# A modulation vector product moved from three blocks in the first layer into 24 steps between the dense chunks of both layers

## The chip, the cores and the metric

The kernel runs on one core of a Trainium2 chip. The metric is the device time of one execution in microseconds (us); lower is better. Engines are named as the profile names them: PE is the matrix engine (PEld its weight loads), DVE the vector engine, ACT the scalar engine, POOL the general one, SP the engine that issues most DMAs. Each engine works through its own list of instructions in order.

## The reference, cut to what matters

Two blocks follow each other. The first has two layers (an RWKV branch, a sparse attention branch "dsa", a dilated attention branch "dil", an output product, a gate). The second has one layer: attention and a gated delta rule, then 16 experts. Only the second block uses the modulation vector `mod`, and `mod` depends on nothing but the input `c` and its weights:

```
x = first_block(x, ...)                        # DEPTH = 2 layers
mod = jax.nn.silu(c) @ w_ada[l] + b_ada[l]     # [1, 1024] @ [1024, 6144], DEPTH_2 = 1
sh1, sc1, gt1, sh2, sc2, gt2 = split(mod, 6)
h  = rmsnorm(x, norm1_w) * (1 + sc1) + sh1
x  = x + gt1 * hybrid_mixer(h, ...)
h2 = rmsnorm(x, norm2_w) * (1 + sc2) + sh2
x  = x + gt2 * expert_choice_ffn(h2, ...)
```

`w_ada` is 25 MB in f32; it is read once, for one row of output. So the product may be made anywhere ahead of the second block.

## The kernel before

All weights of dense products pass through `wring`, four slots of [128, 1024] f32 (`NW = 4`), which `wraw` fills by DMAs from SP. For a product in halves, `w` lets `split` turn a slot into a high and a low f16 part (ACT writes the high one, DVE the low one) in one of `NS = 3` buffers `w`. `fm` makes one **chunk** of 128 features for 512 tokens from such a buffer: 8 times `mm`, three f16 matmuls each, so 24 matmuls of 512 columns into one accumulator tile `bm`. In a layer 29 chunks are made by `fm`: two for the index queries and one for the index keys, one for `wd`, four (`r`, `k`, `v`, `g`) for each of the three head pairs p of the RWKV branch, nine in `dil`, four in `dsa`.

`emit_rwkv` goes over p = 0, 1, 2. For each it makes the four chunks, prepares the operands (lines 428 to 503: transposes `bt`, products `bg`, masked copies), calls `between(p, 1)`, then `solve` (two triangular systems, six levels, line 325), then the state products and the output `y`. `between` also places the index blocks and `dil` by the table `ORDER`. After the branches come the products with `w_out`, the projection `ple_proj`, the norm of the gate and the gate itself (`dense`).

The modulation is made by `Mod.group`, called from `between` by the table `ADA`: in the first layer only, at p = 0, 1, 2, after the preparation and ahead of `solve`. One group makes 4 x 512 outputs: eight times it loads two [128, 1024] f32 pieces of `w_ada` **through `wring`**, and multiplies them by one column of `sc` (silu of c): four f32 matmuls with one output row each, on rows 0, 32, 64 and 96 of one `bm` tile, which runs on over all eight. Then ACT copies the four rows out and SP stores them. `finish`, called after both layers, adds the bias and turns the vector into columns.

The order in which instructions stand is not the order of the code: a scheduler takes them by their place in the code as priority, as soon as it thinks their inputs and buffers are there, and a tile gets its space in SBUF or PSUM when it is scheduled. So the next p's chunks are put between the steps of the present p's `solve`.

## Time and profile before

| | |
|---|---|
| median of 3 runs | 2205.38 us (2202.47 to 2209.64) |
| profiled execution | 2194.62 us |
| its span, first to last instruction | 2192.8 us |
| PE busy | 2017.3 us (92%) |
| DVE busy | 1303.9 us (59%) |
| ACT busy | 962.3 us (44%) |
| moved by DMA | 348.48 MB, mean 159 GB/s |

PE is busy nearly throughout, so the thing to read is, stretch by stretch, what PE does and for what it waits where it doesn't. Matmuls overlap: what one occupies is read from the start of one to the start of the next, not from its own duration. An f32 matmul has two records in the trace. Both layers run the same code but for the groups, so the layers can be laid over each other by a landmark that both have: line 266, which writes the transposed normed input (`hT0H`) at the start of a layer and again at the norm of the gate. "PEclk" is the granted TensorE clock as a share of full speed (its levels are 1.2 and 2.4 GHz).

### The profile page before, as it was taken

How to read it: one execution, taken by the hardware profiler on the slowest of the kernel's cores; microseconds unless marked ns; L12 is line 12 of the kernel's file. 1: busy time of each engine (PE TensorE's matmuls, PEld its weight loads, DVE VectorE, ACT ScalarE, POOL GpSimd, SP SyncE). 2: the span in 40 equal slices, each digit the busy share in tenths (PEclk: the TensorE clock that was granted, in tenths of full speed). 3: DMA queues.
4: the chain of work that ended last, by engine and by line, in shares of the span. 5: the costliest groups of instructions: out<-in, count | busy, mean ns of one | idle time of the engine just before them, and what ended most of it. 6: DMA issues, size and time to landing. Idle time of an engine off the chain costs nothing. (4 is left out here: it accounts for less than half of the span.)

```text
span 2192.8 us, 31685 instructions
## 1 busy us (share of the span) xinstructions
PE 2017.3 (92%) x12269; PEld 1090.4 (50%) x12273; DVE 1303.9 (59%) x2491; ACT 962.3 (44%) x1839; POOL 234.6 (11%) x266
## 2 busy tenths in 40 slices
PE   6898899989989889989799989899996999999998
PEld 4453445444646545444446555565633444444443
DVE  5787966546689986646768576868566112222221
ACT  5454536444555546444667676757521111011010
POOL 0022131000120231000021020302000000000000
PEclk9999999999999999999999999999998999999999
DMA  6344341043321111044221211111067799999996
GB/s 212 125 135 159 110 157 46 14 163 116 98 96 39 39 49 40 12 157 141 79 77 40 67 40 39 54 52 46 30 212 300 303 403 409 409 409 409 408 409 254
DMA packets 114335, 348.48 MB, mean 159 GB/s; under 512 B 19820, under 2 KB 20604, under 8 KB 114184
## 3 DMA queue, kind: packets, MB, share of 16 engines
q1 hardware_dynamic: 110152, 340.51, 42.1%
q10 hardware_dynamic: 4032, 5.95, 0.8%
q8 instruction: 97, 1.59, 0.3%
q14 instruction: 54, 0.44, 0.1%
HBM read 332.70 MB, written 10.56 MB: 157 GB/s over the span
## 5 line engine op out<-in xcount | busy, mean ns | idle before, releaser
L201 PEld LDWEIGHTS <-w 128*128 128x128 f16 x2472 | 232.7, 99 | 240.9 <-issue 35.3
L201 PE MATMUL bm<-hT0H,w 128*128 128x512 f16 x760 | 256.1, 385 | 0.8 <-DVE w L195 0.4
L201 PE MATMUL bm<-hT1H,w 128*128 128x512 f16 x760 | 251.5, 382 | 0.0
L195 DVE SCALAR_TENSOR_TENSOR w<-wring,w 128x1024 f16<-128x1024 f32 x137 | 179.2, 1312 | 22.7 <-ACT w L192 22.1
L1405 PE MATMUL bm<-wm,xe 128*64 128x512 f32 x848 | 185.4, 593 | 0.0
L192 ACT ACTIVATE w<-wring 128x1024 f16<-128x1024 f32 x137 | 144.4, 1059 | 12.7 <-DMA wring<-in_win 8.9
L201 PE MATMUL bm<-hT0L,w 128*128 128x512 f16 x380 | 146.5, 385 | 0.0
L201 PE MATMUL bm<-hT1L,w 128*128 128x512 f16 x380 | 145.6, 383 | 0.0
L1405 PEld LDWEIGHTS bm<-wm,xe 128*64 128x64 f32 x848 | 75.1, 136 | 106.5 <-issue 99.9
L346 DVE TENSOR_TENSOR Z<-bz,perm 128x512 f16<-128x512 f32 x168 | 108.4, 683 | 24.6 <-PE bz L325 23.3
L356 ACT ACTIVATE XX<-bz 128x512 f16<-128x512 f32 x168 | 106.9, 641 | 6.3 <-PE bz L325 6.1
L1382 DVE TENSOR_SCALAR OH<-phA,perm 128x64 f32<-128x64 f32 x128 | 30.1, 308 | 127.4 <-PE bz L1393 96.8
L325 PEld LDWEIGHTS <-XX 128*128 128x128 f16 x1008 | 73.1, 100 | 65.2 <-DVE XX L340 28.5
L1405 PE MATMUL bm<-wm,aT 128*64 128x512 f32 x432 | 102.3, 602 | 0.7
L616 ACT ACTIVATE PT<-bt 128x128 f32<-128x128 f32 (+3 forms) x112 | 47.9, 430 | 118.7 <-PE bt L614 117.4
L353 ACT ACTIVATE XX<-bz 128x512 f16<-128x512 f32 x140 | 90.1, 643 | 14.7 <-PE bz L325 14.4
L1396 ACT ACTIVATE xe<-bz,perm 128x128 f32<-128x128 f32 x64 | 25.8, 453 | 130.2 <-PE bz L1393 118.9
L311 DVE SCALAR_TENSOR_TENSOR hid<-hth,bm 128x512 f32<-128x512 f32 x16 | 10.3, 683 | 115.8 <-ACT hth L310 115.8
L1393 PEld LDWEIGHTS bz<-OH,x 128*128 128x128 f32 x512 | 62.4, 197 | 29.0 <-issue 26.8
L310 ACT ACTIVATE hth<-bm 128x512 f32<-128x512 f32 x16 | 8.7, 595 | 154.4 <-PE bm L1405 154.4
L1393 PE MATMUL bz<-OH,x 128*128 128x128 f32 x512 | 68.6, 287 | 1.7 <-DVE OH L1382 1.7
L325 PE MATMUL bz<-XX,Z 128*128 128x128 f16 x672 | 66.0, 219 | 3.7 <-ACT XX L353 3.6
(517 smaller groups left out, 4046.6 us busy)
## 6 DMA issues: line engine op xcount, KB each, us to landing
wm<-in_w_up SPq DMA_DIRECT2D x112, 512.0 KB, 10.2
wm<-in_w_down SPq DMA_DIRECT2D x108, 512.0 KB, 10.2
wm<-in_w_gate SPq DMA_DIRECT2D x100, 512.0 KB, 10.2
wring<-in_win SPq DMA_DIRECT2D x95, 512.0 KB, 3.3
wring<-in_w_ada SPq DMA_DIRECT2D x48, 512.0 KB, 3.9
wring<-in_w_gate SPq DMA_DIRECT2D x20, 512.0 KB, 10.2
wring<-in_w_down SPq DMA_DIRECT2D x20, 512.0 KB, 9.8
wring<-in_w_out SPq DMA_DIRECT2D x16, 512.0 KB, 5.3
```

The lines of the kernel that those rows point to most:

```text
L192: d = self.A.activation(out=hi, in_=t, func=AF.Copy, scale=scale)
L195: self.V.scalar_tensor_tensor(out=lo, in0=t, scalar=scale, in1=hi, op0=ALU.mult, op1=ALU.subtract)
L201: self.T.matmul(out, a[i], b[j], start=(start and n == 0), stop=(stop and n == 2))
L325: T.matmul(b[:, u], lhs[:, u], rhs if len(rhs.shape) == 2 else rhs[:, u], start=True, stop=True)
L346: V.tensor_tensor(out=z, in0=mm(HL[j][0], X[j]), in1=lv(systems[j], l, 0), op=ALU.mult)
L353: A.activation(out=X[j], in_=mm(XT[j], Z[j]), func=AF.Copy)
L356: A.activation(out=XT[j], in_=b, func=AF.Copy)
L616: K.A.activation(out=PT[:, :n], in_=b[:, :n], func=AF.Copy)
L1382: V.tensor_scalar(out=y[:, t, 64 * e:64 * e + 64], in0=K.c("iota")[:, 1:65], scalar1=slot[:, t, x:x + 1], scalar2=scale(t, x), op0=ALU.is_ ...
L1393: T.matmul(b[:, j], K.x[t][:, (k0 + j) * 128:(k0 + j + 1) * 128], OH[:, t], start=(t == 0), stop=(t == 3))
L1396: A.activation(out=xe[:, k], in_=b[:, j], func=AF.Identity, scale=n2[:, k:k + 1], bias=modc[:, 24 + k:25 + k])
L1405: T.matmul(bb[hf][s], lhs[:, k, s], w[:, hf * 512:(hf + 1) * 512], start=(k == 0), stop=(k == 7))
```

## The change

`ADA` and `Mod.group` are gone. `fm` calls `Mod.tick` after each chunk, and every second tick is a `step`: it multiplies the pieces that were loaded by the step before (four f32 matmuls), and starts the two loads for the next step. There are 24 steps (three groups of eight k as before), all in the two layers of the first block. The pieces go into tiles `aw` of their own ([128, 2, 1024] f32, two buffers) and no longer through `wring`. Each load is made to wait (`K.after`) for the last matmul of the chunk behind which it stands. `finish` would do what is left over.

```
--- before.py
+++ after.py
@@ -28,7 +28,6 @@
 NS = 3
 ND = 4
 ORDER = {(0, 0): ("1",), (1, 0): ("2",), (2, 0): ("3",), (2, 1): ("dil",), "end": ("dsa", "fin")}
-ADA = {(0, 0, 1): (0,), (0, 1, 1): (1,), (0, 2, 1): (2,)}
 NM = 24
 NM1 = 8
 NC = 4
@@ -198,7 +197,8 @@
     def mm(self, out, a, b, start, stop):
 
         for n, (i, j) in enumerate(((0, 0), (0, 1), (1, 0))):
-            self.T.matmul(out, a[i], b[j], start=(start and n == 0), stop=(stop and n == 2))
+            d = self.T.matmul(out, a[i], b[j], start=(start and n == 0), stop=(stop and n == 2))
+        return d
 
     def wm(self, src, pool):
 
@@ -278,7 +278,8 @@
 
         b = (pool or self.pm).tile([128, 512], F32, name="bm", bufs=4)
         for k in range(8):
-            self.mm(b, tuple(w[:, k * 128:(k + 1) * 128] for w in wt), hT[k], k == 0, k == 7)
+            d = self.mm(b, tuple(w[:, k * 128:(k + 1) * 128] for w in wt), hT[k], k == 0, k == 7)
+        self.mod.tick(d)
         return b
 
     def rope_fm(self, sp, b, cos, sin, mask, out, perm=None, half=None, scale=1.0):
@@ -835,8 +836,6 @@
     later.update(dil=dil, dsa=dsa, **{str(b): (lambda b=b: block(b)) for b in (1, 2, 3)})
 
     def between(p, end):
-        for n in ADA.get((i, p, end), ()):
-            K.mod.group(sp, n)
         for n in ORDER.get((p, end), ()):
             later[n]()
 
@@ -912,6 +911,7 @@
 class Mod:
 
 
+
     def __init__(self, K):
         A, V = K.A, K.V
         self.K = K
@@ -922,25 +922,42 @@
         V.tensor_scalar(out=self.sc, in0=self.sc, scalar1=0.5, scalar2=None, op0=ALU.mult)
         self.c = K.small("modc", 48)
         self.scr = K.dp.tile([12, 512], F32, name="mod")
-
-    def group(self, sp, g):
-
+        self.n, self.calls, self.w = 0, 0, None
+
+    def tick(self, mark):
+        self.calls += 1
+        if self.calls % 2:
+            self.step(mark)
+
+    def step(self, mark=None):
         K = self.K
-        b = K.pm.tile([128, 512], F32, name="bm", bufs=4)
-        for k in range(8):
-            w = [K.wraw(K.a["w_ada"][k * 128:(k + 1) * 128, m * 1024:(m + 1) * 1024]) for m in (2 * g, 2 * g + 1)]
+        if self.w is not None:
+            g, k = divmod(self.n - 1, 8)
+            if k == 0:
+                self.b = K.pm.tile([128, 512], F32, name="bm", bufs=4)
             for j in range(4):
-                d = K.T.matmul(b[32 * j:32 * j + 1], self.sc[:, k:k + 1], w[j // 2][:, (j % 2) * 512:(j % 2) * 512 + 512],
-                               start=(k == 0), stop=(k == 7))
-                if j < 2:
-                    K.after(d, K.wlast)
-        row = sp.tile([128, 512], F32, name="modrow")
-        for j in range(4):
-            K.A.activation(out=row[32 * j:32 * j + 1], in_=b[32 * j:32 * j + 1], func=AF.Copy)
-            K.nc.sync.dma_start(self.scr[4 * g + j:4 * g + j + 1], row[32 * j:32 * j + 1])
+                K.T.matmul(self.b[32 * j:32 * j + 1], self.sc[:, k:k + 1], self.w[:, j // 2, (j % 2) * 512:(j % 2) * 512 + 512],
+                           start=(k == 0), stop=(k == 7))
+            if k == 7:
+                row = K.wp.tile([128, 512], F32, name="modrow")
+                for j in range(4):
+                    K.A.activation(out=row[32 * j:32 * j + 1], in_=self.b[32 * j:32 * j + 1], func=AF.Copy)
+                    K.nc.sync.dma_start(self.scr[4 * g + j:4 * g + j + 1], row[32 * j:32 * j + 1])
+            self.w = None
+        if self.n < 24:
+            g, k = divmod(self.n, 8)
+            self.w = K.wp.tile([128, 2, 1024], F32, name="aw", bufs=2)
+            src = K.a["w_ada"][k * 128:(k + 1) * 128, g * 2048:(g + 1) * 2048].rearrange("p (m n) -> p m n", m=2)
+            for m in range(2):
+                d = K.nc.sync.dma_start(self.w[:, m], src[:, m])
+                if mark is not None:
+                    K.after(d, mark)
+            self.n += 1
 
     def finish(self, sp):
 
+        while self.n < 24 or self.w is not None:
+            self.step()
         K = self.K
         m48 = sp.tile([128, 512], F32, name="modrow")
         K.nc.sync.dma_start(m48[0:48, 0:128], self.scr.rearrange("a (b c) -> (a b) c", b=4))
```

Order on SP, first layer. `wring<-in_win` is the load of one chunk's weights, `wring<-in_w_ada` or `aw<-in_w_ada` that of one piece for the modulation, `mod<-modrow` the store of a finished row. Before, from the first group to the third:

```order
L175 DMA wring<-in_win 128x1024 x2
L175 DMA wring<-in_w_ada 128x1024 x16
L175 DMA wring<-in_win 128x1024 x3
L940 DMA mod<-modrow 1x512 x4
L175 DMA wring<-in_win 128x1024
L175 DMA wring<-in_w_ada 128x1024 x16
L175 DMA wring<-in_win 128x1024 x4
```

The change, around the end of its first eight steps:

```order
L952 DMA aw<-in_w_ada 128x1024 x2
L174 DMA wring<-in_win 128x1024 x2
L952 DMA aw<-in_w_ada 128x1024 x2
L945 DMA mod<-modrow 1x512 x4
L174 DMA wring<-in_win 128x1024
L952 DMA aw<-in_w_ada 128x1024 x2
L174 DMA wring<-in_win 128x1024 x4
```

Sixteen loads in a row in the chunks' ring became single pairs, in buffers of their own, with one to four chunk loads between them.

Order on PE, first layer, head pair 0, the preparation of `solve`. `L933` is the group; `bt<-perm,AR` and so on are the preparation's transposes. Before:

```order
L933 MATMUL bm<-wring,perm 1x512
L436 MATMUL bg<-wd,lv 128x512
L443 MATMUL bg<-sq,perm 128x512
L933 MATMUL bm<-wring,perm 1x512 x7
L591 MATMUL bs<-ik,iqs 128x384 x3
L933 MATMUL bm<-wring,perm 1x512 x4
L591 MATMUL bs<-ik,iqs 128x384
L933 MATMUL bm<-wring,perm 1x512
L386 MATMUL bt<-perm,AR 128x128 x4
L933 MATMUL bm<-wring,perm 1x512 x3
```

The change, at the transposes; `L200` is a matmul of a chunk (the second one of head pair 1):

```order
L387 MATMUL bt<-perm,AR 128x128 x4
L200 LDWEIGHTS w
L200 MATMUL bm<-hT1H,w 128x512
L387 MATMUL bt<-perm,bh 128x128 x4
L200 LDWEIGHTS w
L200 MATMUL bm<-hT1H,w 128x512
L387 MATMUL bt<-perm,kh 128x128 x2
L466 MATMUL bg<-rz,perm 128x512
L387 MATMUL bt<-perm,kh 128x128 x2
L387 MATMUL bt<-perm,vz 128x128 x4
```

What stood between the instructions of the preparation was the group; now it is the next head pair's chunk. A step stands where that chunk began (`bm_1548` and `bm_1587` are the first and second chunk of head pair 1, `bm_498` is the modulation's accumulator):

```order
L200 MATMUL bm_1548<-hT1H_151,w_1545 128x512
L939 MATMUL bm_498<-aw_861,perm_82 1x512 x4
L200 LDWEIGHTS w_1584
L200 MATMUL bm_1587<-hT0H_149,w_1584 128x512
L200 LDWEIGHTS w_1584
```

Four matmuls of the modulation stand together between two chunks, where before up to twelve stood together. Over the whole program the 96 matmuls stand in 29 runs on PE before and in 30 in the change (24 steps, of which six are parted into one and three); 15 steps stand in the first layer and 9 in the second.

## Rows read from the trace of the kernel before

**Rows 1.** Page, busy time: engine, us (share of the span), instructions.
```profile
PE 2017.3 (92%) x12269; PEld 1090.4 (50%) x12273; DVE 1303.9 (59%) x2491; ACT 962.3 (44%) x1839; POOL 234.6 (11%) x266
```

**Rows 2.** Windows: both layers between landmarks, then the three preparations beside the groups.
```profile
core 0: us, PE busy (x) PEld busy (x) DVE busy (x) ACT busy (x) POOL busy (x), PEclk, DMA share, GB/s
17.90:501.50 483.60, 443.18 (x2735) 234.34 (x2738) 342.96 (x652) 228.48 (x455) 70.07 (x72) 0.95 0.36 116
557.20:997.10 439.90, 405.32 (x2545) 230.72 (x2546) 329.79 (x652) 225.32 (x448) 70.49 (x72) 0.97 0.21 70
60.00:112.60 52.60, 44.74 (x194) 19.48 (x192) 37.89 (x83) 20.34 (x39) 5.81 (x5) 0.87 0.39 130
167.90:198.60 30.70, 25.67 (x113) 9.37 (x112) 23.85 (x42) 15.66 (x30) 7.93 (x7) 0.89 0.42 137
252.40:279.80 27.40, 19.91 (x91) 6.87 (x89) 21.68 (x34) 15.25 (x27) 7.84 (x7) 0.81 0.58 192
```

**Rows 3.** Line 266: count, ns min/median/max, first to last start us; four stretches.
```profile
L266 ACT ACTIVATE hT0H<-bt x4: 575/597/597, 17.9 to 28.5; 128x512 f16<-128x512 f32 x4
...
L266 ACT ACTIVATE hT0H<-bt x4: 597/597/616, 501.5 to 510.4; 128x512 f16<-128x512 f32 x4
...
L266 ACT ACTIVATE hT0H<-bt x4: 591/597/597, 557.2 to 565.2; 128x512 f16<-128x512 f32 x4
...
L266 ACT ACTIVATE hT0H<-bt x4: 597/597/597, 997.1 to 1008.0; 128x512 f16<-128x512 f32 x4
```

**Rows 4.** Line 933, the groups' matmuls, and PE busy with it in a window.
```profile
L933 PE MATMUL bm<-wring,perm x192: 589/591/1061, 95.1 to 293.1; 128*1 128x512 f32 x192
...
60.00:300.00 240.00, 40.26 (x192) 3.94 (x192) 0.93 0.43 141
```

**Rows 5.** PE's waits, layer 0 (first row), layer 1: total us, times, longest.
```profile
PE bm L933 <- DMA wring<-in_w_ada: 19.1, 11, 3.8
...
PE bg L465 <- DVE rz L463: 5.1, 2, 2.9
...
PE bs L591 <- ACT rl L593: 0.9, 2, 0.8
```

**Rows 6.** Timeline of PE, groups 0 and 1: start us, duration us, what.
```profile
98.14 1.89 PE L933 MATMUL bm<-wring,perm 128*1 128x512 f32 x14
99.96 0.79 PE L591 MATMUL bs<-ik,iqs 96*128 96x384 f32 x3
...
186.22 1.04 PE L933 MATMUL bm<-wring,perm 128*1 128x512 f32 x8 [0.63 <-DMA wring<-in_w_ada]
187.19 0.50 PE L591 MATMUL bs<-ik,iqs 96*128 96x512 f32 x1
```

**Rows 7.** Timeline of PE inside a dense chunk.
```profile
84.17 0.59 PE L201 MATMUL bm<-hT0H,w 128*128 128x512 f16 x2
84.60 0.38 PE L201 MATMUL bm<-hT0L,w 128*128 128x512 f16 x1
```

**Rows 8.** Landing of chunk loads, then modulation loads; the two halves of a split.
```profile
DMA to landing us min/median/max: 3.1/3.3/8.4
...
DMA to landing us min/median/max: 3.6/3.9/6.2
...
L192 ACT ACTIVATE w<-wring x46: 1039/1049/1256, 15.8 to 534.5; 128x1024 f16<-128x1024 f32 x46
L195 DVE SCALAR_TENSOR_TENSOR w<-wring,w x46: 1202/1220/2296, 16.9 to 536.0; 128x1024 f16<-128x1024 f32 x46
```

**Rows 9.** Page, costliest groups: reading of an accumulator in `solve`; busy, mean ns, idle.
```profile
L346 DVE TENSOR_TENSOR Z<-bz,perm 128x512 f16<-128x512 f32 x168 | 108.4, 683 | 24.6 <-PE bz L325 23.3
L356 ACT ACTIVATE XX<-bz 128x512 f16<-128x512 f32 x168 | 106.9, 641 | 6.3 <-PE bz L325 6.1
```

**Rows 10.** Line 939, the copies of finished rows.
```profile
L939 ACT ACTIVATE modrow<-bm x12: 569/587/589, 130.6 to 296.2; 1x512 f32<-1x512 f32 x12
```

**Rows 11.** Windows, all engines, in the experts' stage.
```profile
1800.00:2000.00 200.00, 194.91 (x955) 92.19 (x952) 41.18 (x98) 21.31 (x46) 0.00 (x0) 1.00 1.03 409
```

## Prediction

> **What bounds the kernel now.** I read the page's busy times first: PE is busy 92% of the span, DVE 59%, ACT 44% [rows 1]. So a microsecond counts where PE works or waits. The modulation is made in the first layer only, and both layers run the same code otherwise, so the second reading lays one layer over the other. The landmark is line 266, which starts a layer and comes again at the norm of the gate: 17.9 to 501.5 us in the first layer, 557.2 to 997.1 in the second [rows 3]. The windows between these landmarks give 483.60 us with 443.18 of PE for the first layer and 439.90 with 405.32 for the second [rows 2]. The first is 43.7 us longer: 37.9 us of PE work, and 5.8 of idle PE (40.4 against 34.6). The third reading is line 933, the groups: 192 records (two for each of 96 matmuls), 40.26 us of PE [rows 4], which is about the difference in work; and in the list of PE's waits it waited 19.1 us, eleven times, for pieces of `w_ada`, up to 3.8 at once [rows 5]. So PE gave the modulation 40.26 + 19.1 = 59.4 us, and the layer got 43.7 longer: 15.7 us of it, a share of 0.26, lay in time in which PE would have stood still anyway. The second layer shows that time: PE waits there for DVE and ACT in the preparation of `solve`, 5.1 us of it at line 465 [rows 5].
>
> The fourth reading is the clock. In the three preparations beside the groups the granted clock is 0.87, 0.89 and 0.81 of full speed, over a layer 0.95 and 0.97 [rows 2]: between the waits for pieces PE fell to its lower level, 1.2 GHz, for part of the time, and its matmuls, the groups' own among them, took twice as long there.
>
> **The change part by part.**
>
> *The groups go.* If nothing of the modulation were left in the first layer, it would look like the second: 43.7 us less. This takes their work, their waits, the clock that they cost, and their seizing of the chunks' ring together, and it rests on the two layers being alike otherwise.
>
> *The steps come.* Four matmuls that stand together write four different groups of 32 rows, and overlap: such a step runs from 186.22 to the next instruction at 187.19, 0.97 us [rows 6]. Parted into one and three, as six of the 24 are in the new order, it takes two such passes. So 30 passes x 0.97 = 29.1 us. That is less than the 40.26 of before, where the order has 34 passes (29 runs, long ones in several passes): 40.26 / 34 = 1.18 each, the lower clock in it.
>
> Two passes in one run took 98.14 to 99.96, 1.82 us [rows 6], so the second cost 0.85 and entering cost 0.12. The Trainium skill, "TensorEngine Tiling (Array Packing)", Key Properties, says that going from one tiling of the array to another drains it, which speaks against strewing these matmuls among full-width ones; the 0.12 agrees with it. Without such a price the steps would be 30 x 0.85 = 25.5 us, with it 29.1. The sum takes the row's 0.97.
>
> *What of the steps is hidden.* Bounds: nothing (29.1 us on the path) and all of it (PE stands idle 34.6 us in the second layer's window alone). I take the share that the groups had, 0.26, the only row of the same work in the same surroundings: 7.6 us, so 21.5 on the path. A step stands mostly between two chunks, where PE is dense and nothing is hidden, but nine of them stand in the second layer, ahead of products that wait.
>
> *The loads.* Count and bytes stay (two pieces for each of 24 products, before and after). A piece lands 3.6 to 6.2 us after its issue, median 3.9 [rows 8]. It is issued when a chunk ends and used two chunks later; a chunk is 24 matmuls at 0.216 (two in 0.43) [rows 7], 5.2 us, so 10.4 us of PE lie between at least. So the 19.1 us of waits should go. If that cover were gone, a step would wait up to the 3.8 us of before. What is queued behind a held-back load on SP: the chunks' loads, then `iqy`, `mod` and `w_out`. The ring's four slots and three split buffers let seven chunks be ahead, 36 us of PE, and a chunk load that would overtake the mark has to wait for about the same chunk to free a split buffer. So I cost the hold-back at nothing; without this cover a late chunk load is 3.3 us of landing and 1.05 + 1.22 of splitting [rows 8], 5.6 us each.
>
> *The rest.* ACT still copies twelve rows, 12 x 0.587 = 7.0 us [rows 10], and SP stores them; four of the copies come in the second layer, beside chunks, and ACT is busy 225 of 440 us there [rows 2]. `finish` has its product in the second layer and not long before; its rows are wanted by the norm that opens the second block, after two more dense products. Both at nothing; if that cover is gone, a few us once. The accumulator is held over eight steps, some sixteen chunks, no longer over one group: that is the second rival. The second block is carried along: the experts' stage has the DMA engines full at 409 GB/s and PE busy 195 of 200 us [rows 11], and its loads start behind marks of the stage ahead, so it starts sooner by what the layers gain and takes as long as before.
>
> *Sum.* 43.7 - 21.5 = 22.2 us. The profiled execution, 2194.62, becomes 2172.4. The median of the runs shown is 10.8 above that execution, so the median becomes 2205.4 - 22.2 = **2183 us**. With none of the steps hidden the gain is 14.6 (2191), with all of it 43.7 (2162). The idle time gives a check: work falls by 40.26 - 29.1 = 11.2, the rest of the 22.2 is 11.0 of idle PE out of 75.0 in both windows, less than the 19.1 that pieces cost.
>
> **Rivals.**
>
> *Exposed and dear.* The steps cost what a pass cost on average before, 1.18 us, and hide nothing: 30 x 1.18 = 35.4, gain 8.3, **2197 us**. For it: they stand where PE is dense. Against: the 1.18 has the low clock in it, which came with waits that go.
>
> *The held accumulator (slower).* One `bm` tile is taken from the chunks, `solve` and attention from the second step to the last, across nearly two layers, while before it was taken three times for some 36 us each (line 933 begins at 95.1, line 939 at 130.6) [rows 4, 10]. In `solve` PE writes an accumulator as soon as ACT or DVE has read what was there, 0.64 and 0.68 us each [rows 9]. If PE waits for one such reading more at each level, that is six solves x six levels x 0.64 = 23 us, and the gain is gone: 2206. If it waits for each of the two systems, 46 us: 2183 + 46 = **2229 us**. It decides from one wait a level upward. Against: PE's waits have hardly one that ends with a tile being read for reuse (0.9 us at line 591 is the clearest) [rows 5].
> The Trainium skill, "PSUM — Partial Sum Buffer", Specifications, gives eight banks of 512 f32 values a partition, so the held tile would be one of eight for everything; no run here counts banks.
>
> *The hold-back holds too much.* The change's own wait does not do what it says: SP stands at a piece whose mark is later than the scheduler thought, and chunk loads behind it come late. Each time costs up to 5.6 us; four times in 24 eat the gain: **2205 us**. For it: SP works strictly in order, and now has 24 such places. Against: the seven chunks of lead.
>
> *More hidden.* The steps fill idle time wholly, since the scheduler may put them anywhere after their pieces: gain 43.7, **2162 us**. Against: 24 single places are fixed in PE's order, and 15 of the steps stand whole in front of a dense chunk.
>
> **How the numbers follow.** About 0.3% (6.6 us) is what a measurement can tell from no change. Chances: the forecast (2176 to 2191) 0.55; exposed and dear 0.12, half of which I count within 0.3%; the accumulator 0.12, all slower; the hold-back 0.10, within 0.3%; more hidden 0.11. So faster 0.55 + 0.06 + 0.11 = 0.72, within 0.3% 0.16, slower 0.12. The range goes from the last rival to the hold-back's end, 2162 to 2206; what it leaves out is the accumulator's case and a little at the lower end.
>
> **What would show it.** In the profile of the changed kernel: the steps' line has 192 records, busy 29 us (35 if they are dear), and nearly no wait for `aw`. The window from line 266 to line 266 is about 440 + 18 x 0.97 x 0.74 = 453 us in the first layer (18 passes stand there) and 440 + 12 x 0.97 x 0.74 = 449 in the second. The granted clock in the first layer's preparations is that of the second's. It would be wrong if PE's waits in `solve`, lines 325 and 364, grew by more than 10 us (the accumulator), if waits for `w` at line 201 showed up (the hold-back), or if the time after the second layer changed by more than 5 us, which no step of this sum foresees.

## The result, and the profile of the changed kernel

The changed kernel takes 2151.51 us in the median of four runs (2142.93 to 2155.46); the kernel before, beside it, 2207.1 (2202.47 to 2209.64). The ratio is 0.9745, with an interval of 0.9721 to 0.977. So it is 55.6 us faster, where 22 were forecast, and faster than the low end of the range (2162). The profiled execution of the changed kernel took 2155.46 us, with a span of 2153.7; beside [rows 2] and the 2194.62 of before that is a gain of 39.2.

The windows of the changed kernel, from one landmark to the next (columns as in [rows 2]: length, then busy time of PE, PEld, DVE, ACT and POOL, granted clock, DMA share, GB/s). The first two rows are the layers, the others cut each layer where the last `y` of the branches is copied out of PSUM: the branches ahead of it, then what I call the closing part: the attention of `dsa` and the output of `dil`, with the products of `w_out` between.

```profile
17.20:461.70 444.50, 417.07 (x2664) 231.69 (x2665) 339.26 (x657) 228.72 (x451) 68.98 (x72) 0.97 0.33 108
518.40:955.00 436.60, 415.53 (x2619) 232.15 (x2620) 332.58 (x650) 230.45 (x456) 72.24 (x72) 0.97 0.27 90
...
17.20:359.30 342.10, 319.51 (x2149) 185.67 (x2150) 282.67 (x524) 179.76 (x340) 66.95 (x70) 0.97 0.33 106
359.30:461.70 102.40, 97.57 (x516) 46.02 (x515) 56.60 (x133) 48.96 (x111) 2.03 (x2) 0.98 0.33 115
518.40:857.90 339.50, 321.63 (x2120) 187.04 (x2121) 275.89 (x526) 181.38 (x344) 70.21 (x70) 0.96 0.26 82
857.90:955.00 97.10, 93.90 (x500) 45.10 (x499) 56.69 (x125) 49.07 (x112) 2.03 (x2) 1.00 0.33 120
```

The same cuts in the kernel before:

```profile
17.90:389.90 372.00, 339.60 (x2243) 186.26 (x2244) 285.89 (x520) 180.51 (x345) 68.04 (x70) 0.95 0.39 125
389.90:501.50 111.60, 103.58 (x493) 48.09 (x494) 57.08 (x133) 47.97 (x111) 2.03 (x2) 0.94 0.25 87
557.20:887.30 330.10, 305.82 (x2064) 183.77 (x2063) 276.10 (x537) 178.16 (x339) 67.52 (x70) 0.97 0.18 57
887.30:997.10 109.80, 99.50 (x482) 46.94 (x483) 53.68 (x116) 47.16 (x110) 2.97 (x2) 0.95 0.31 110
```

Read them in pairs. The first layer's branches fell from 372.0 to 342.1, the second's rose from 330.1 to 339.5: together -20.5, near what the forecast had for the whole change (22.2). The closing parts fell from 111.6 to 102.4 and from 109.8 to 97.1: together -21.9, and no term of the forecast stands for that. Two of the 24 steps stand in the first closing part (8 matmuls, 3.1 us of PE) and none in the second. What is left (start, gates, second block) grew by 3.3; -20.5 - 21.9 + 3.3 is the 39.1 by which the spans differ.

The steps themselves, in the changed kernel's tile view (count, duration in ns min/median/max, first to last start in us) and in the page's list of DMA issues (count, KB each, median us from issue to landing):

```profile
L939 PE MATMUL bm<-aw,perm x192: 590/591/592, 49.6 to 763.0; 128*1 128x512 f32 x192
...
aw<-in_w_ada SPq DMA_DIRECT2D x48, 512.0 KB, 4.7
```

PE is busy with this line for 18.63 us up to 530 and 12.39 after it, 31.0 together, and no wait of PE for `aw` is in the trace; before, it waited 19.1 us for pieces [rows 5].

### The profile page after: what moved, and what is told of

The parts are those of the page before. It is cut to its first block, busy times and chain, and to the rows that moved or that the text cites. A ratio compares the mean times of both kernels' runs of the same rounds, so it can differ in the third digit from the quotient of the medians.

```text
span 2153.7 us, 31719 instructions
## 1 busy us (share of the span) xinstructions
PE 2009.9 (93%) x12273; PEld 1094.1 (51%) x12273; DVE 1300.1 (60%) x2491; ACT 965.6 (45%) x1840; POOL 236.4 (11%) x266
## 5 line engine op out<-in xcount | busy, mean ns | idle before, releaser
L200 PEld LDWEIGHTS <-w 128*128 128x128 f16 x2472 | 231.3, 99 | 252.9 <-issue 51.9
L200 PE MATMUL bm<-hT0H,w 128*128 128x512 f16 x760 | 258.1, 388 | 0.1
L200 PE MATMUL bm<-hT1H,w 128*128 128x512 f16 x760 | 251.6, 381 | 0.0
L194 DVE SCALAR_TENSOR_TENSOR w<-wring,w 128x1024 f16<-128x1024 f32 x137 | 174.1, 1277 | 25.1 <-ACT w L191 24.9
L191 ACT ACTIVATE w<-wring 128x1024 f16<-128x1024 f32 x137 | 143.8, 1057 | 30.1 <-PE bm L200 22.7
L200 PE MATMUL bm<-hT0L,w 128*128 128x512 f16 x380 | 147.5, 388 | 0.0
L200 PE MATMUL bm<-hT1L,w 128*128 128x512 f16 x380 | 144.4, 380 | 0.0
L312 DVE SCALAR_TENSOR_TENSOR hid<-hth,bm 128x512 f32<-128x512 f32 x16 | 10.3, 684 | 107.4 <-ACT hth L311 107.4
```

The lines of the kernel that those rows point to most:

```text
L191: d = self.A.activation(out=hi, in_=t, func=AF.Copy, scale=scale)
L194: self.V.scalar_tensor_tensor(out=lo, in0=t, scalar=scale, in1=hi, op0=ALU.mult, op1=ALU.subtract)
L200: d = self.T.matmul(out, a[i], b[j], start=(start and n == 0), stop=(stop and n == 2))
```

## The experiments

The question from the first reading: is the closing parts' 21.9 us an effect of its own, or one of the modulation's move, or of the clock from one execution to another? **Theory A**: there are two gains, and the second comes from the sequence in which PE takes the closing part's products; the scheduler arrived at another one because tiles were held differently. **Theory B**: there is one gain, the modulation's, and the closing parts vary for other reasons.

All times of stages below come from windows like those above. "Idle" is a window's length less PE's busy time; "low clock" is busy time x (1 - granted clock), what the lower level (1.2 GHz instead of 2.4) cost. Both are sums over the two closing parts. "Both heads" counts, of a layer's eight steps of `dsa`, those in which PE's order has the transposes of both heads ahead of the first head's product with v (first layer, second layer). "Rest" is the span less these four stages and the time ahead of the first. The median of before is that beside the changed kernel; each ratio goes against runs of before on the same chip (medians 2203.5 to 2207.1). Times in us.

| kernel | branches 1, 2 | closing 1, 2 | idle | low clock | both heads | rest | profiled span | median | ratio (interval) |
|---|---|---|---|---|---|---|---|---|---|
| before | 372.0, 330.1 | 111.6, 109.8 | 18.3 | 11.2 | 0, 0 | 1251.4 | 2192.8 | 2207.1 | 1 |
| changed | 342.1, 339.5 | 102.4, 97.1 | 8.0 | 2.0 | 5, 5 | 1255.4 | 2153.7 | 2151.5 | 0.9745 (0.9721-0.977) |
| e1 no product | 336.6, 331.5 | 112.0, 102.0 | 17.3 | 11.4 | 0, 0 | 1265.0 | 2165.2 | 2169.8 | 0.9834 (0.9796-0.9872) |
| e2 held tile | 373.3, 328.6 | 99.8, 97.3 | 6.7 | 0.0 | 4, 5 | 1246.8 | 2162.5 | 2163.8 | 0.9806 (0.9775-0.9838) |
| e3 released tile | 349.8, 342.9 | 107.4, 104.5 | 15.0 | 4.9 | 0, 0 | 1268.3 | 2190.5 | 2191.8 | 0.9944 (0.992-0.9969) |
| e4 every chunk | 361.0, 326.2 | 92.8, 94.7 | 5.4 | 0.0 | 5, 5 | 1259.0 | 2153.3 | 2155.3 | 0.977 (0.9733-0.9807) |
| e5 spread | 376.0, 322.6 | 117.7, 115.0 | 16.3 | 19.5 | 0, 0 | 1255.8 | 2205.2 | 2216.8 | 1.0056 (1.0032-1.0079) |
| e6 own ring | 361.1, 328.4 | 100.4, 97.6 | 8.6 | 2.9 | 5, 6 | 1266.6 | 2171.9 | 2177.4 | 0.987 (0.9834-0.9905) |
| e7 chunks' ring | 351.1, 360.6 | 98.2, 109.2 | 7.6 | 11.5 | 5, 5 | 1255.9 | 2191.7 | 2194.0 | 0.9955 (0.9935-0.9974) |
| e8 no hold-back | 345.3, 335.4 | 109.2, 109.0 | 16.4 | 10.0 | 0, 0 | 1268.1 | 2185.1 | 2187.5 | 0.9929 (0.9898-0.996) |
| e9 row forced | 377.2, 324.4 | 110.4, 95.5 | 8.9 | 9.4 | 5, 5 | 1253.2 | 2178.6 | 2182.5 | 0.9899 (0.9857-0.9941) |
| e10 row back | 342.1, 336.4 | 112.3, 119.6 | 17.4 | 13.0 | 0, 0 | 1248.4 | 2176.6 | 2172.3 | 0.9858 (0.982-0.9895) |

**e1: no product.** The kernel before without the modulation's product; zeros go to the second block.

```
-ADA = {(0, 0, 1): (0,), (0, 1, 1): (1,), (0, 2, 1): (2,)}
+ADA = {}
...
+        z = K.wp.tile([128, 512], F32, name="modrow")
+        V.memset(z[0:12], 0.0)
+        K.nc.sync.dma_start(self.scr, z[0:12])
```

> The kernel before without the modulation's product: no load of its weights, no group, zeros in its place, all else as it is. Closing part = from the last y of a layer (line 548, p = 2) to the norm of the gate (line 266); before 111.6 and 109.8 us, changed kernel 102.4 and 97.1. Branch part = from line 266 at a layer's start to that y; before 372.0 and 330.1, changed kernel 342.1 and 339.5. Theory A (two gains: the groups leave the branch part, and the closing parts are ordered differently because the change holds one accumulator for two layers): the closing parts stay at 108 to 112 us, the first branch part comes to 330 to 340, the time is 40 to 45 us below before, 2162 to 2167, so above the changed kernel's 2151 although it does less. Theory B (one gain: the modulation cost more than counted, and with it gone the closing parts are faster too): closing parts about 102 and 97, time 60 us or more below before, about 2145.

The groups cost the first layer's branches 372.0 - 336.6 = 35.4 us, not 43.7; against this kernel the steps cost the branches 5.5 and 8.0, 13.5 together. And a kernel without any product takes 2169.8, longer than the changed kernel that makes it. Taking the product away cannot explain the whole gain. The closing part of the first layer stays at 112.0. That of the second does not: it is 102.0, the length that theory B gave, though its order is still one head at a time and its idle PE 8.6 us. What differs there from before is the clock, which was full throughout. The time, too, lies above the 2162 to 2167 of theory A, since the rest is 13.6 us longer than before.

**e2: held tile.** The kernel before with one `bm` tile (a PSUM bank) taken at the start and given back behind the 49th dense chunk; the modulation stays in its three groups.

```
+        self.hb = K.pm.tile([128, 512], F32, name="bm", bufs=4)
+        K.T.matmul(self.hb[0:8, 0:8], self.sc, self.sc, start=True, stop=True)
...
+    def tick(self, mark):
+        self.calls += 1
+        if self.calls == 49:
+            self.K.after(self.K.V.tensor_copy(self.K.small("hp", 8)[0:8], self.hb[0:8, 0:8]), mark)
```

> The kernel before with its groups as they are, and one more PSUM tile bm that is written once at the start and read after the 49th chunk, where the changed kernel ends its last step; nothing else. In PE's order the longest runs of attention matmuls in the closing parts without a product between them go from 38, 27 and 38, 38 to 20 and 19, 18 (changed kernel: none of 14 or more, and 19, 18). Theory A: closing parts about 102 and 97 us, branch parts as before (372, 330), time about 20 us below before, 2187. Theory B: no gain, 2207, or some us slower for the lost tile.

The rival that I feared as slower makes the kernel before 40 us faster, by itself; theory A had expected 20. The branches are as before; the closing parts are 99.8 and 97.3, and their clock is full:

```profile
390.00:489.80 99.80, 96.03 (x510) 46.45 (x509) 63.11 (x142) 50.67 (x114) 3.74 (x3) 1.00 0.30 107
...
875.60:972.90 97.30, 94.35 (x501) 45.37 (x501) 56.60 (x126) 48.72 (x111) 2.03 (x2) 1.00 0.33 119
```

In the second closing part the tile is no longer held (it is read at 779.9 us). So a missing bank cannot be what acts there; what is left is the sequence at which the scheduler has arrived by then. Of the median's 40 us the closing parts' windows show 24.3; the rest of this gain lies in the part after the layers (-4.6 in the table) and in the clock from one execution to another (below).

**e3: released tile.** The changed kernel, each step with an accumulator of its own that is given back at once; DVE adds the eight up in SBUF. To that end each product writes 32 rows instead of one (its column of `sc` is padded with 31 columns of zeros).

```
-            if k == 0:
-                self.b = K.pm.tile([128, 512], F32, name="bm", bufs=4)
+            b = K.pm.tile([128, 512], F32, name="bm", bufs=4)
...
+            if k == 0:
+                K.V.tensor_copy(self.acc[g], b)
+            else:
+                K.V.tensor_tensor(out=self.acc[g], in0=self.acc[g], in1=b, op=ALU.add)
```

> The changed kernel, but each step has an accumulator of its own, which DVE adds into SBUF at once (24 additions of about 0.68 us) and which is free again then. The runs of attention matmuls in the closing parts are long again: 35, 21 and 35, 32. Theory A: closing parts 108 to 112 us each, branch parts like the changed kernel's, time some 20 us above the changed kernel, 2170. Theory B: as the changed kernel, 2151, give or take 5.

Most of the gain goes: 2191.8, 22 us above what theory A expected. The branches lose 11.1 to the changed kernel, the closing parts 12.4 (107.4 and 104.5, below the 108 to 112 expected), the rest 12.9. The run does more than give a bank back: it adds 24 operations of DVE and tiles in SBUF, so the loss is not the price of the release alone.

**e4: every chunk.** The changed kernel with a step at every dense chunk and not at every second, so that all 24 fall into the first layer.

```
-        if self.calls % 2:
+        if self.calls > 0:
```

> The changed kernel with a step after every chunk and no longer after every second, so that all 24 stand in the first layer. Both theories: the first branch part 6 to 9 us longer than the changed kernel's 342, the second back to about 330, time within 8 us of the changed kernel's 2151. Theory A alone: the tile is not held in the second layer, and its closing part lies between 97 and 110 us (its runs of attention matmuls are 21, 16, 14, those of the first layer 21, 16).

The time is that of the changed kernel (2155.3 against 2151.5). The branches pay 18.9 us in the first layer, where 6 to 9 were expected, for 13.3 gained in the second, and the closing parts are the shortest of all, 92.8 and 94.7. So it matters little for the sum in which layer the steps stand, and the closing parts are fast without a step in the second layer.

**e5: spread.** First try at the sequence itself: the kernel before, with `w_out`'s products for its first half of columns and three groups of channels tied to steps of `dsa`.

```
...
+                if spread and not hf and k < 3 and spread[4 * k + t] >= 0:
+                    self.after(d1, self.steps[spread[4 * k + t]])
...
+    K.dense(yS, a["w_out"][i], residual, spread=[-1, -1, 0, 1, 1, 2, 2, 3, 3, 4, 4, 5])
```

> The kernel before with one thing added: in the closing part of each layer the products of w_out for the first half of its columns and the first three groups of input channels each wait for one step of the last attention's two passes (orders in place of a rush of filler at one end), so that TensorE's row there holds no run of attention steps longer than 23, where the kernel before has 38. The modulation is not touched: its three groups stand where they stood. Theory A (two gains; the second is the order of the closing parts): the closing parts, from the last y copy of the branches to the gate's first product, fall from 111.6 and 109.8 us to 95 to 105 each, the branches stay at 372 and 330 (within 6), and the time falls by 15 to 30 us, ratio 0.986 to 0.993. Theory B (the gain is the modulation's alone; closing parts vary with the clock from run to run): the closing parts stay within 5 us of 110 and the time within 8 us of before, ratio 0.997 to 1.003.

A miss: slower, closing parts of 117.7 and 115.0. This did not make the changed kernel's sequence: the heads still come one behind the other (0, 0), and products held back were missing where PE had nothing else. The windows of the first closing part show it:

```profile
404.00:408.00 4.00, 4.00 (x22) 1.73 (x20) 3.65 (x5) 2.50 (x4) 0.74 (x1) 1.00 0.24 66
408.00:412.00 4.00, 1.33 (x5) 0.53 (x4) 3.41 (x13) 1.06 (x4) 0.00 (x0) 1.00 0.12 38
412.00:416.00 4.00, 3.41 (x10) 1.40 (x10) 1.40 (x5) 1.25 (x6) 0.00 (x0) 0.54 0.00 0
416.00:420.00 4.00, 4.00 (x10) 1.36 (x8) 0.81 (x3) 0.84 (x3) 0.00 (x0) 0.50 0.00 0
420.00:424.00 4.00, 3.85 (x13) 1.76 (x13) 1.40 (x4) 0.95 (x3) 0.00 (x0) 0.50 0.00 0
424.00:428.00 4.00, 4.00 (x9) 1.32 (x9) 0.00 (x0) 0.22 (x1) 0.00 (x0) 0.50 0.00 0
```

PE works at full clock, then only 1.33 us of four, and then has some 16 us at a granted clock of 0.50, although it is busy nearly all of them. The wait cost 2.7 us and the lower clock about 8. The measure I had used, the longest run of attention products without a product of `w_out` between, was wrong; "both heads" in the table came out of this miss.

**e6: own ring.** The kernel before, its groups still blocks, but their weights in two buffers of their own.

```
-            w = [K.wraw(K.a["w_ada"][k * 128:(k + 1) * 128, m * 1024:(m + 1) * 1024]) for m in (2 * g, 2 * g + 1)]
+            aw = K.wp.tile([128, 2, 1024], F32, name="aw", bufs=2)
+            w = [aw[:, 0], aw[:, 1]]
+            for m in range(2):
+                e = K.nc.sync.dma_start(w[m], K.a["w_ada"][k * 128:(k + 1) * 128, (2 * g + m) * 1024:(2 * g + m + 1) * 1024])
...
-                    K.after(d, K.wlast)
+                    K.after(d, e)
```

> The kernel before, its three groups of the modulation still blocks of 16 passes in layer 0's branches, but with the weights in a ring of their own (two buffers of 2 x 1024) instead of the ring of the chunks' raw weights. It tells the cost of the seized ring from that of the block. If the groups' cost in the first layer's branches (372.0 us with them, 336.6 with the product left out) was mostly the chunks' weights coming late behind them: branches of layer 0 at 342 to 352. If it was the wait of the block for its own weights and the passes: 360 to 372. By theory A the closing parts go by their order, which the reservation changes: runs of attention steps without filler of 21, 16 and 14 in the first layer and 30, 24, 21 and 14 in the second, between before and after, so 100 to 108 each. By theory B they stay at 110. Time by theory A 2165 to 2190, by theory B 2180 to 2200.

The ring is worth 10.9 us in the first layer's branches (372.0 to 361.1), so of the two ranges it is the second: most of the groups' cost there is the block's own waits and passes. The other 19.0 of the changed kernel's 29.9 need the steps. The closing parts are short here too, with a sequence of "both heads" and without a tile held in PSUM: another change of the buffers, the same turn of the order.

**e7: chunks' ring.** Meant as the changed kernel with its pieces in the chunks' ring.

```
...
-            self.w = K.wp.tile([128, 2, 1024], F32, name="aw", bufs=2)
+            self.w = []
...
-                d = K.nc.sync.dma_start(self.w[:, m], src[:, m])
-                if mark is not None:
-                    K.after(d, mark)
+                self.w.append(K.wraw(src[:, m], 1, mark))
```

> The changed kernel with its 24 steps, but their weights through the chunks' raw ring instead of a ring of their own. It tells what the ring of its own is worth when the product is in steps. Theory A: each step takes two of the ring's buffers while a chunk's weights wait for them, but at most one step is in flight, so the branches lose little: layer 0 at 342 to 352 (after: 342.1), layer 1 at 339 to 349 (after: 339.5); closing parts by their order, 95 to 105. Time 2150 to 2175. Rival (the own ring is the gain): the branches come to 355 to 375 in layer 0 and 2185 to 2200 in all.

The run says little. The ring of four slots goes round before a step's product is issued, so that many of the products read slots that a chunk's weights have taken over: loads and products are as many as meant, but products wait for other loads than `w_ada`'s. I take no price of the ring from it. Its second closing part has "both heads" and 5.0 us of idle PE, and is still 109.2 long, 11.5 of it at the lower clock.

**e8: no hold-back.** The changed kernel without the mark on the loads of `aw`.

```
-                if mark is not None:
-                    K.after(d, mark)
```

> The changed kernel without the hold-back: the loads of the steps' weights are issued as soon as one of the ring's two buffers is free. It tells what the hold-back is worth, and tests the order again: without the mark, the closing parts' order again has runs of attention steps of 24 and 14 in the first layer and 38 and 35 in the second. Theory A: branches as after (342 and 339, within 6 us), closing part of the second layer back at 105 to 110 (after: 97.1) and of the first at 100 to 105, time 2158 to 2175. Theory B (closing parts don't go by the order): 2150 to 2160. Rival (the hold-back itself earns, since early loads collide with the chunks' weights): branches 350 to 360.

The branches are those of the changed kernel (345.3 and 335.4; 342.1 and 339.5), so by itself the hold-back neither costs nor earns there. But the sequence turns back to one head at a time, the closing parts to 109.2 and 109.0, and the rest grows by 12.7: 2187.5, longer than I had expected of either theory. One line of code that moves no work costs 36 us: 18.7 of them stand in the closing parts, 8.3 in the second block, whose order moved too (below).

**e9 and e10: the sequence forced.** Here the 172 attention products and 96 products of `w_out` of each closing part are tied into a row, by orders that need no semaphore. e9 is the kernel before with the changed kernel's row, e10 the changed kernel with the row of before. No other order is given (`ROW` is the list of their places; every product passes through a recorder, so that the trace gives its line, 740 or 741, for all of them).

```
+    K.T.rec = []
     for n in ORDER["end"]:
         later[n]()
...
     K.dense(yS, a["w_out"][i], residual)
+    rec, row = K.T.rec[-364:], [j for s, n in ROW[i] for j in range(s, s + n)]
+    for j, k in zip(row, row[1:]):
+        K.tc.add_manual_dep(rec[k].ins, rec[j].ins.name, mybir.DependencyInfo(mybir.DependencyClass.NoSync, mybir.DependencyReason.SCHED_ONLY),
+                            reason="row")
```

> The kernel before with one thing added: in the closing part of each layer the 172 attention products and the 96 products of w_out's first half are held, by orders without a semaphore, in exactly the sequence in which the changed kernel has them (both heads' transposes ahead of the first head's product with v, and w_out's products strewn through to the end of the attention). No tile is held, no ring added, and the modulation stands in its three groups. Theory A (the second gain is this sequence): closing parts from 111.6 and 109.8 us to 96 to 104 each; idle TensorE in the two from 18.3 to 6 to 11 us, and the time lost there to a clock under full speed from 10.7 to 0 to 4; branches as before (372.0 and 330.1, within 8); time 2175 to 2190, ratio 0.988 to 0.994. Theory B (the closing parts got faster by something else: the held accumulator itself, the state of the clock): closing parts 107 and more, time within 8 us of before.

> The changed kernel with the closing parts' 268 products of each layer held in the sequence of the kernel before (one head's transposes, its copy, its product, then the other head). The modulation stands in its 24 steps, with the ring and the hold-back. Theory A: closing parts from 102.4 and 97.1 back to 106 to 114 each, idle TensorE there from 8 to 15 to 20; branches as in the changed kernel (342.1 and 339.5, within 8); time 2165 to 2182. Theory B: closing parts stay at 97 to 103, time 2148 to 2158.

Both come out within the times that theory A gave. e9: 2205.2 to 2182.5, -22.7, with the modulation untouched. PE's order in its second block is that of before, product for product; in the branches it shifted, and their times moved by +5.2 and -5.7, which cancel. e10: 2172.3, 20.8 above the changed kernel (measured beside different runs of before, but the intervals of the two ratios lie apart), with branches within 3.1 us of it. By stage, e10 is plain: closing parts of 112.3 and 119.6 (the second above the 106 to 114 expected), and PE again waits for the copy of the transposes, here in the second (engine, line, releaser, then us, times, longest):

```profile
PE bo L741 <- ACT PT L617: 6.7, 9, 2.6
```

In e9 the second closing part is 95.5, the shortest but e4's, and the first is a half miss: 110.4, where 96 to 104 were expected. Its idle time fell by 1.6, but one wait of 2.67 us for DVE stands near its head, and behind it the clock was at its lower level:

```profile
410.00:415.00 5.00, 2.42 (x10) 0.94 (x10) 3.99 (x13) 2.39 (x10) 0.00 (x0) 0.82 0.00 1
415.00:420.00 5.00, 5.00 (x11) 1.85 (x12) 0.00 (x0) 0.77 (x2) 0.00 (x0) 0.50 0.00 0
420.00:425.00 5.00, 5.00 (x17) 1.85 (x16) 2.13 (x6) 1.23 (x4) 0.00 (x0) 0.66 0.00 0
...
412.57 0.52 PE L740 MATMUL bt<-perm,P 128*128 128x128 f32 x2 [2.67 <-DVE P L611]
...
395.10:505.50 110.40, 103.96 (x506) 49.02 (x507) 58.18 (x139) 49.90 (x113) 2.40 (x2) 0.91 0.25 87
885.70:981.20 95.50, 93.09 (x497) 44.86 (x496) 55.72 (x122) 49.18 (x112) 2.04 (x2) 1.00 0.35 128
```

So theory A holds for the time and for the idle PE, with both signs, and theory B falls. Of the clock it holds less well: e9's first closing part lost 9.4 us to it where 0 to 4 were expected in both. Over the twelve kernels, the closing parts with one head at a time have 6.8 to 10.3 us of idle PE each and last 102.0 to 119.6; those with both heads have 2.3 to 6.4, and last 92.8 to 102.4 where the lower clock took under 4 us (the two others are e7's second and e9's first). The sequence shows in the idle time of all 24 parts, though narrowly in e9's first (6.4 us); the lower clock goes with it in most, not in all (e1's second, one head at a time, had none). Of the 21.9 us between before and the changed kernel, 10.3 are idle time and 9.2 the lower clock.

**What the sequence does** is seen in PE's timeline (start us, us, then in brackets the idle time before it and who ended it). The kernel before, last step of `dsa` in the second layer:

```profile
935.65 0.87 PE L640 MATMUL bo<-PT,v 128*64 128x128 f32 x10 [0.36 <-ACT PT L616]
937.13 0.63 PE L614 MATMUL bt<-perm,P 128*128 128x128 f32 x4 [0.61 <-DVE P L611]
938.51 0.64 PE L640 MATMUL bo<-PT,v 128*64 128x128 f32 x2 [0.75 <-ACT PT L616]
939.90 1.12 PE L614 MATMUL bt<-perm,P 128*128 128x128 f32 x4 [0.75 <-DVE P L611]
940.81 0.42 PE L614 MATMUL bt<-perm,DP 128*128 128x128 f32 x1
941.70 1.97 PE L640 MATMUL bo<-PT,v 128*64 128x128 f32 x14 [0.47 <-ACT PT L616]
...
935.00:940.00 5.00, 2.53 (x19) 1.39 (x18) 1.99 (x5) 2.42 (x6) 0.00 (x0) 0.86 0.01 3
940.00:945.00 5.00, 4.53 (x24) 3.15 (x24) 0.69 (x1) 1.04 (x3) 0.00 (x0) 0.50 0.00 0
```

The changed kernel, the same step:

```profile
902.70 0.66 PE L615 MATMUL bt<-perm,P 128*128 128x128 f32 x4
903.19 0.59 PE L200 MATMUL bm<-w,yS 128*128 128x512 f16 x2
903.62 0.60 PE L615 MATMUL bt<-perm,P 128*128 128x128 f32 x4
904.15 0.43 PE L641 MATMUL bo<-PT,v 128*64 128x128 f32 x2
904.52 0.33 PE L615 MATMUL bt<-perm,DP 128*128 128x128 f32 x1
904.68 0.59 PE L200 MATMUL bm<-w,yS 128*128 128x512 f16 x2
905.21 1.09 PE L641 MATMUL bo<-PT,v 128*64 128x128 f32 x14
```

Before, each product with v comes right behind the transposes whose copy it needs, and PE stands until ACT has made that copy; each head's transposes stand until DVE has scaled P. Then PE, half idle from 935 to 940, works at the lower clock from 940 to 945, and the 14 small products take 1.97 us instead of 1.09. In the changed kernel the other head's transposes or products of `w_out` stand between, and nothing waits: 3.6 us from the first transposes to the end of the products, before 6.5.

**The order of the second block moved as well.** These are its attention and delta rule, from line 266 after the second layer to the first product row with `w_o` (columns as above): before, changed kernel, e8.

```profile
1063.20:1643.10 579.90, 544.14 (x3958) 326.04 (x3958) 402.88 (x703) 368.33 (x680) 87.01 (x114) 0.97 0.20 68
...
1019.60:1603.90 584.30, 550.22 (x3951) 329.18 (x3951) 403.73 (x701) 370.21 (x680) 88.11 (x114) 0.96 0.20 66
...
1040.00:1632.60 592.60, 547.78 (x3961) 325.06 (x3961) 407.69 (x702) 378.09 (x686) 88.28 (x114) 0.97 0.19 66
```

PE takes this stretch in the same order, product for product, in e1, e3, e6 and e8, and there it lasts 592.3 to 593.6 us, 44.0 to 44.8 of them idle. In before, e5 and e9 the order is another one, again the same in all three, and it lasts 579.9 to 583.7, with 35.8 to 36.9 idle. So most of the 14 to 17 us by which the rest of e1, e3, e6 and e8 exceeds that of before lies here, where no edit touched a product. No run forces this order, so that it is the cause is argued from the grouping and not shown.

## Why the prediction was wrong, step by step

The prediction's mechanism for the modulation was there, but a second gain of the same size was missing, and the time lies outside the range. Three steps failed.

**The step that failed first: an order that changes was priced only where the modulation stands.** The forecast gave 453 and 449 us for the layers; they are 444.5 and 436.6. The missing 8.5 and 12.4 are nearly the closing parts' 9.2 and 12.7. "The rest" had ACT's copies, the product of `finish`, the accumulator and the second block in it, and no term for the attention of the closing parts, whose rows in PE's order had changed as well. The forecast took the two layers as "alike otherwise", and that what stands behind them would be carried along; in this kernel the order of both layers and of the second block came out anew when a buffer was held longer. e9 and e10 show 21 to 23 us for that in the medians, with both signs.

**The accumulator's rival had the wrong sign.** It expected a wait per level of `solve`. In the first layer's branches of the changed kernel the waits in `solve` are small; these are the largest wait there and the largest in `solve` (line 326):

```profile
PE bt L387 <- DVE AR L459: 8.0, 3, 4.5
...
PE bz L326 <- DVE XX L341: 0.8, 1, 0.8
```

By e2 the held tile alone makes the kernel before 40 us faster, and in e3, which releases it, most of the gain is lost. The Trainium skill, "PSUM — Partial Sum Buffer", Specifications, gives eight banks, which speaks for the rival. No run here shows a wait that a missing bank causes.

**The conversion from one execution to the median.** I added the 10.8 us between the profiled execution of before and its median to the new time, as if they were a property of both kernels. They were one of that execution: it had a mean granted clock of 0.969 and 2194.62 us, while the 38 that ran beside e1 to e10 had 0.956 to 0.966 and 2193.49 to 2215.74, with medians of 2203.5 to 2205.2. The changed kernel's profiled execution is the slowest of its four (0.971, 2155.46; the fastest 0.976, 2142.93). So the profiled pair shows 39.2 and the medians 55.6: 12.5 of the difference are before's distance from its median, 3.9 the changed kernel's, on the other side. Against e10, whose closing parts have the sequence of before, 2205.2 - 2172.3 = 32.9 are left for the modulation's move in the medians. The windows of the branches show 20.5 of that (23.6 in e10); where the medians' other 9 to 12 lie is not shown, since each window is of one execution.

**The two terms of the sum** were both too large, and it is luck that their errors nearly cancel (35.4 - 13.5 = 21.9, beside 22.2). The groups: 35.4 instead of 43.7 in the branches, since the layers are not alike without them (e1: 336.6 and 331.5, and 112.0 and 102.0 in the closing parts, 11.4 of the former at the lower clock). The steps: 13.5 instead of 21.5 on the path. Their work was nearly right, 31.0 us busy against 29.1. But 3.1 of it stands in the first closing part, and of the 27.9 in the branches 27.9 - 13.5 = 14.4 are hidden, a share of 0.52 and not the 0.26 of the groups. A block that stands in one place can hide only in that place's idle time. Idle PE in the branches fell by 9.8 us in the first layer (32.4 to 22.6) and 6.4 in the second (24.3 to 17.9); it lies 1.6 and 7.6 below that of e1, which has no product. So the steps fill gaps, most of them in the second layer. (The run at 98.14 that the forecast read as two passes of a step has 14 records, so it is three matmuls and then four; the sum does not rest on it.)

**What was right.** The 19.1 us of waits for pieces are gone; nothing waits for `aw`. The hold-back costs the branches nothing (e8). PE's waits in `solve` did not grow. The granted clock over the branches, 0.95 and 0.97 before, is 0.97 and 0.96. The time after the second layer changed by 4.5 us (1129.6 to 1134.1), inside the 5 that I allowed; 4.4 of it are the second block's attention and delta rule, whose order moved, so that it was only 4.5 is luck.

**What stays open.** Why the scheduler turns from one sequence to the other: a held bank does it (e2), a ring of its own without a held bank does it (e6), the same ring without the hold-back does not, although a bank is held (e8), nor does it with the bank released (e3, which has other changes as well). I know of no rule that would have told it without building the kernel. Why the mean clock of one program differs from execution to execution is open as well, and so is what the second block's order costs by itself. A kernel with e4's closing parts and the changed kernel's branches would by the table gain some 12 us more, an estimate (199.5 - 187.5); it was not run, and e4 itself is no faster than the changed kernel.

## What to carry to other kernels

Where a scheduler sets the order, a change of a buffer can change the order everywhere: compare the order of every stage before pricing, and give each stage whose order moved a term of its own, with both signs. Look in PE's order for a product that stands right behind the step whose copy it needs: it pays the wait, and here often the lower clock on top. Another head's work between left less idle PE in every kernel that had it, and less of the lower clock in most; the order can be pinned by hand (e9) instead of being left to luck. Price a change from the medians of several executions, or at least note the granted clock of the one that was profiled.

## What the runs showed of the hardware that was not expected

A short stand of PE was followed by a loss of up to three times its own length. In e5, 2.7 us of missing work in four were followed by some 16 us at a granted clock of 0.50, some 8 us lost; in e9 a stand of 2.67 us was followed by stretches at 0.50 and 0.66. In the prediction the clock was a matter of the waits for pieces, up to 3.8 us long; here shorter stands were followed by it too, but not every one. In the kernel before, in the first closing part, PE was 1.69 us busy of four, and the clock stayed at 1.00 (windows, columns as above):

```profile
444.00:448.00 4.00, 1.69 (x15) 0.99 (x12) 1.31 (x5) 1.53 (x5) 0.00 (x0) 1.00 0.01 4
448.00:452.00 4.00, 3.36 (x28) 2.18 (x28) 0.69 (x1) 1.64 (x5) 0.00 (x0) 1.00 0.00 0
```

The time of one program, the kernel before, differed by 22 us between 21 executions on one chip (2193.57 to 2215.74, mean granted clock 0.956 to 0.965), as much as the gain that was forecast.
